# Two projections of a transformer layer by Strassen's identity, on one Trainium2 core

## The chip, the core and the metric

The kernel runs on one core of one Trainium2 chip. TensorE (PE) does the matrix products into PSUM; VectorE (DVE), ScalarE (ACT) and GpSimd (POOL) do everything elementwise; SyncE (SP) issues the weight DMAs. The metric is device microseconds of one execution of the whole layer, as a median over runs. All numbers are fp32 or fp32r.

## The reference

One layer on x of 512 rows and 1024 columns. The front part of it (three kinds of attention and gating, with their gates) is not touched by the change; what matters is the two projections behind it, each followed by a residual sum and a layer norm:

```python
merged = gates_a * (oa @ w_proj_a) + gates_b * (ob @ w_proj_b) + gates_c * (oc @ w_proj_c)
y = merged @ w_out                                   # 512x1024 @ 1024x1024
h = layer_norm(ALPHA * x + y, ln1_g, ln1_b)
a, bval = split(h @ w_ffn_up, 2)                     # 2816 columns each
a = causal_conv3(a, conv_w) + conv_b
y = (gelu(a) * bval) @ w_ffn_down                    # 512x2816 @ 2816x1024
out = layer_norm(ALPHA * h + y, ln2_g, ln2_b)
```

## The kernel before

**Splits.** Every product is computed from operands that are split into a high part (rounded, on ACT) and a low part (the rest, on DVE), and is the sum of three matmuls: high by low, low by high, high by high (`mm3_ops` L214, `mm3` L220). One step of 128 contraction rows, 128 output rows and 512 output columns is therefore three matmuls.

**The weight stream.** `emit_load` (L108) issues a DMA of 1 MB on SP into one of three raw buffers; `emit_split` (L119) makes `wh` on ACT (L133) and `wl` on DVE (L134) for units of 1024 values per partition, and `unit()` (L141) asks for them two units ahead. The left operand stands transposed in SBUF (contraction on the partitions): `m` for the output projection, split at L775 (`mTh`) and L776 (`mTl`) as each of its eight tiles is merged; for the down projection `h2`, split in `up_end` (L902) as each of its 22 tiles is made.

**Projections.** `project` (L816) holds all eight PSUM banks: 4 row blocks of 128 rows by 2 column halves. The early contraction steps run over all eight banks with one unit of weight; the last six steps (`last_rows` L798) are kept split in SBUF (`lh`, `ll`), so that the row blocks finish one after the other. Behind each block DVE adds the product to the residual (L838, `h`), takes statistics (L846, L847), POOL computes the power -0.5 (L649), and four DVE operations of 512 columns finish the norm (L851, L855). After the first projection each block of `h` is then transposed on PE (`th`, L873) and split into `hTh` and `hTl`, which the up projection multiplies (`up`, then `pa` and `pb`). After the second one each block is stored.

**Order.** The order of instructions on each engine is set ahead of time by a scheduler that works from its own times; on the chip each engine runs its list strictly in order, and waits on semaphores where an operand is not there.

Of the kernel before, what the change touches and what calls it, by code (L numbers as in the profile page):

```python
# [19 lines left out]
P = 128  # L20
# [29 lines left out]
def bucket_rows():  # L50
    """Per dilation group the bucket (one-hot, rows 0-31) and the mask (row 32) of each diagonal."""
# [18 lines left out]
def layer_kernel(  # L70
# [6 lines left out]
    big = ctx.enter_context(tc.tile_pool(name="big", bufs=17))  # L77
    wraw = ctx.enter_context(tc.tile_pool(name="wraw", bufs=3))
# [15 lines left out]
    # ---------------------------------------------------------------- weight stream  # L94
# [11 lines left out]
    raws = {}  # L106

    def emit_load():  # L108
# [4 lines left out]
        t = wraw.tile([P, 2048], F32, tag="raw", name=f"raw{n}")  # L113
# [5 lines left out]
    def emit_split():  # L119
# [4 lines left out]
        while state["load"] <= n:  # L124
            emit_load()
        src = f(raws[n])
        a = src.shape[1]
# [7 lines left out]
        prepared[u] = (h3, l3)  # L135
        state["split"] += 1
# [4 lines left out]
    def unit():  # L141
# [5 lines left out]
        while state["load"] <= min(n + 2, len(loads) - 1):  # L147
            emit_load()
        return prepared.pop(u)
# [5 lines left out]
    def kcols(w, k0, nk, c0, nc_):  # L155
        """Rows k0*128.., a [128, nk, nc_] load in units of 1024 per partition."""
# [36 lines left out]
    def krows(w, k, split):  # L193
        add_load([P, 2, 1024], w[k * P:(k + 2) * P, :].rearrange("(k p) c -> p k c", p=P),
                 [lambda r: r[:, 0:1, :], lambda r: r[:, 1:2, :]] if split else [])

    LAST = 6
    n_wout = len(loads) + (KD - LAST) // 2
    for k in range(0, KD, 2):
        krows(wo, k, k < KD - LAST)  # L200
# [9 lines left out]
    n_wdn = len(loads) + (NF - LAST) // 2  # L210
    for k in range(0, NF, 2):
        krows(wdn, k, k < NF - LAST)

    def mm3_ops(ps, w, v, first, last):  # L214
        """ps += w.T @ v for operands split into (hi, lo)."""
# [13 lines left out]
    # ---------------------------------------------------------------- x, transposed and split  # L229
# [41 lines left out]
    # ---------------------------------------------------------------- small parameters  # L271
# [62 lines left out]
    # ---------------------------------------------------------------- q, k, v  # L334
# [87 lines left out]
    # ---------------------------------------------------------------- attention pieces  # L422
# [527 lines left out]
```

## Time and profile before

| what | value |
| --- | --- |
| median of 3 runs | 822.05 us (822.04 to 822.73) |
| span of the profiled execution | 820.5 us |
| busy: PE, DVE, ACT, POOL | 807.0, 382.5, 284.4, 20.4 us |
| output projection on PE | 405.3 to 450.9 us |
| down projection on PE | 693.1 to 812.7 us |

The page gives of the profiled execution only its span; the median of the runs is 1.55 us longer, since some time lies around the span. Rows of the trace have microseconds from the start of the span. PE's busy time counts overlapped matmuls, so the distance from start to start is what a matmul costs.

### The profile page before, as it was taken

Reading aid. Unit: us, or ns where it says so; the run is one execution under the profiler, and the core shown is the slowest. Engines: PE = TensorE matmul, PEld = TensorE weight load, DVE = VectorE, ACT = ScalarE, POOL = GpSimd, SP = SyncE. Lnnn points to the kernel's source line nnn. Section 1 sums busy time; section 2 is a strip of 40 time slices with the busy share of each in tenths; the row PEclk is TensorE's granted clock in tenths of the full one; section 3 lists DMA queues with packets and bytes.
Section 4 is the critical chain, followed back from the end, with each engine's and each line's share of the span. In section 5 each row is a group of like instructions: output and inputs, shape, how many; then the busy total and the mean of one; then the engine's idle time right before and its main releaser. Section 6 shows DMA issues by size and latency. Waiting matters only on the chain.

```text
span 820.5 us, 9700 instructions
## 1 busy us (share of the span) xinstructions
PE 807.0 (98%) x4051; PEld 675.0 (82%) x4051; DVE 382.5 (47%) x591; ACT 284.4 (35%) x433; POOL 20.4 (2%) x32
## 2 busy tenths in 40 slices
PE   7999999999999999999999999999999999999996
PEld 6878997778877788888888988888888888888884
DVE  4333235836664334335856455544454445225055
ACT  4331246665365222223611243333333333224000
POOL 2001000100000000000000000000000000000000
PEclk9999999999999999999999999999999999999998
DMA  9355331122402133242840023233333324224002
GB/s 317 124 196 182 103 129 52 52 78 82 150 26 78 52 103 128 78 152 89 323 154 1 1 103 102 103 103 103 103 103 102 103 83 131 94 102 154 1 26 77
DMA packets 62411, 87.10 MB, mean 106 GB/s; under 512 B 1994, under 2 KB 50154, under 8 KB 62368
## 3 DMA queue, kind: packets, MB, share of 16 engines
q1 hardware_dynamic: 60960, 82.32, 29.5%
q0 software_dynamic: 1408, 4.17, 1.5%
q8 instruction: 32, 0.52, 0.3%
q14 instruction: 11, 0.09, 0.0%
HBM read 84.36 MB, written 4.47 MB: 108 GB/s over the span
## 4 chain that ended last, share of the span: by engine, by line
PE 98%; DMA 1%; DVE 0%; SPq 0%; issue 0%; DVEq 0%
PE y L220 20%; PE gate L220 16%; PE pa L220 13%; PE pb L220 13%; PE qk L220 7%; PE zb L220 6%; PE proj L220 5%; PE v L220 4%; PE up L220 3%; PE oT L524 1%; PE sc L524 1%; PE qc L220 1%; PE pt L493 1%; PE qk L362 1%; PE vc L220 1%; PE kc L220 1%
## 5 line engine op out<-in xcount | busy, mean ns | idle before, releaser
L134 DVE TENSOR_TENSOR wl<-raw,wh 128x1024 fp32r<-128x1024 f32 (+1 forms) x127 | 154.1, 1214 | 186.5 <-ACT wh L133 177.7
L133 ACT ACTIVATE wh<-raw 128x1024 fp32r<-128x1024 f32 (+1 forms) x127 | 133.2, 1050 | 192.9 <-PE pb L220 47.2
L220 PE MATMUL y<-wh,h 128*128 128x512 f32 x256 | 79.0, 389 | 0.0
L220 PE MATMUL gate<-xTh,wl 128*128 128x512 f32 x192 | 76.7, 400 | 0.0
L220 PE MATMUL gate<-xTh,wh 128*128 128x512 f32 x192 | 75.0, 390 | 0.0
L220 PE MATMUL gate<-xTl,wh 128*128 128x512 f32 x192 | 74.9, 390 | 0.0
L220 PE MATMUL pa<-hTh,wl 128*128 128x512 f32 x160 | 62.3, 389 | 0.0
L220 PE MATMUL pa<-hTl,wh 128*128 128x512 f32 x160 | 62.3, 389 | 0.0
L220 PE MATMUL pa<-hTh,wh 128*128 128x512 f32 x160 | 62.2, 389 | 0.0
L220 PE MATMUL pb<-hTh,wl 128*128 128x512 f32 x160 | 62.2, 389 | 0.0
L220 PE MATMUL pb<-hTl,wh 128*128 128x512 f32 x160 | 62.2, 389 | 0.0
L220 PE MATMUL pb<-hTh,wh 128*128 128x512 f32 x160 | 62.2, 389 | 0.0
L220 PEld LDWEIGHTS y<-wh,h 128*128 128x128 f32 x256 | 48.0, 188 | 10.1
L220 PE MATMUL y<-wl,h 128*128 128x512 f32 x128 | 49.8, 389 | 0.0
L898 DVE SCALAR_TENSOR_TENSOR c<-pa,par,c 128x511 f32<-128x511 f32 x20 | 15.0, 750 | 65.8 <-ACT c L897 65.8
L220 PEld LDWEIGHTS gate<-xTh,wl 128*128 128x128 f32 x192 | 36.1, 188 | 8.6 <-issue 1.2
L220 PEld LDWEIGHTS gate<-xTh,wh 128*128 128x128 f32 x192 | 36.0, 188 | 7.8
L897 ACT ACTIVATE c<-pa,par 128x512 f32<-128x512 f32 x20 | 15.6, 781 | 76.1 <-PE pa L220 76.1
L220 PEld LDWEIGHTS gate<-xTl,wh 128*128 128x128 f32 x192 | 36.1, 188 | 7.0
L220 PE MATMUL qk<-xTh,wl 128*128 128x512 f32 (+1 forms) x96 | 35.8, 374 | 0.0
L220 PE MATMUL qk<-xTh,wh 128*128 128x512 f32 (+1 forms) x96 | 35.7, 371 | 0.0
L220 PE MATMUL qk<-xTl,wh 128*128 128x512 f32 (+1 forms) x96 | 35.6, 372 | 0.0
(219 smaller groups left out, 1480.8 us busy)
## 6 DMA issues: line engine op xcount, KB each, us to landing
raw<-in_w_ffn_up SPq DMA_DIRECT2D x22, 1024.0 KB, 4.9
raw<-in_w_in SPq DMA_DIRECT2D x13, 1024.0 KB, 5.0
raw<-in_w_gate SPq DMA_DIRECT2D x12, 1024.0 KB, 5.0
raw<-in_w_ffn_down SPq DMA_DIRECT2D x11, 1024.0 KB, 4.7
raw<-in_w_out SPq DMA_DIRECT2D x4, 1024.0 KB, 4.7
shear<-vecs POOLq DMA_DIRECT2D x1, 2304.0 KB, 14.1
raw<-in_w_mem_kv SPq DMA_DIRECT2D x2, 1024.0 KB, 5.3
raw<-in_w_proj_b SPq DMA_DIRECT2D x4, 512.0 KB, 3.3
```

The costliest lines, as they stand in the source:

```text
L133: nc.scalar.activation(h3, src, AF.Copy)
L134: nc.vector.tensor_tensor(l3, src, h3.bitcast(F32), op=ALU.subtract)
L220: nc.tensor.matmul(ps, w, v, start=first, stop=last)
L362: nc.tensor.matmul(ps[:, sl], w[a][:, k, :], xs(k0 + k, sl)[c], start=k0 + i + k == 0, stop=k0 > 0 and i == 2 and k == 3)
L493: nc.tensor.transpose(pt[:, kb, u, :], self.p[:, u, kb * P:(kb + 1) * P], ident)
L524: nc.tensor.matmul(ps, w, v, start=first, stop=last)
L897: nc.scalar.activation(c, pa, AF.Identity, bias=CB(i), scale=CW(2, i))
L898: nc.vector.scalar_tensor_tensor(c[:, 1:], pa[:, :S - 1], CW(1, i), c[:, 1:], op0=ALU.mult, op1=ALU.add)
```

## The change

Both projections are computed with seven products of half-size quarters instead of eight (Winograd's form of Strassen's identity). The left operand A is cut into quarters by rows (0 to 255, 256 to 511) and by contraction (even and odd blocks of 128); the weight B by the same contraction and by columns (0 to 511, 512 to 1023). `PHASES` lists the seven products, each a left quarter or sum (S1 to S4) by a weight quarter or sum (T1 to T4); `a`, `d` and `e` are pairs of PSUM banks that sum up over phases and are added into `h` with a plus or minus sign as the phases end (`done`, L902, `add`, L900).

The weight sums are made in place on POOL (L234 to L243) in operations of 128x1024, before the split into `wh` and `wl` (L142, L143). Two of the left sums are made on POOL when the left operand is ready (`left_sums`, L824 and L825), the others are updates on DVE (L835, L838). The left operand is no longer split as it is produced: each unit in each phase splits its own left quarter into `ah` (ACT, L287) and `al` (DVE, L289 or L291), 512 values per partition. Instead of 64 steps the output projection has 56 (168 matmuls for 192), and the down projection 154 for 176 (462 for 528). The weights are loaded whole by quarters; the raw buffers come from the pool `big`, which has 20 buffers for 17, and the separate pool of three goes. Operations of 512 columns that add a bank into `h` are 14 for each projection instead of 8.

```diff
-    mTh = [T8(f"mTh{i}", F32R) for i in range(2)]
-    mTl = [T8(f"mTl{i}", F32R) for i in range(2)]
+    PHASES = (
+        ("a", "A11", "B11"), ("d", "S1", "T1"), ("a", "S2", "T2"), ("d", "S4", "B22"),
+        ("a", "S3", "T3"), ("e", "A12", "B21"), ("a", "A22", "T4"),
+    )
...
+            if q == "T1":
+                t = quarter("B11", j, n)
+                nc.gpsimd.tensor_tensor(t, t, quarter("B12", j, n), op=ALU.add)
...
+                def left_parts(u, left=left, j=j, n=n):
+                    src, scale = lefts[name](left, j, n)
+                    ah = work.tile([P, 2, 256], F32R, tag="ah", bufs=3, name=f"ah{u}")[:, :n, :]
+                    al = work.tile([P, 2, 256], F32R, tag="al", bufs=3, name=f"al{u}")[:, :n, :]
+                    split_of(ah, al, src, scale)
...
+    def left_sums(t, z, n):
+        nc.gpsimd.tensor_tensor(z, left_block(t, "A21", n), left_block(t, "A22", n), op=ALU.subtract)
+        nc.gpsimd.tensor_tensor(left_block(t, "A21", n), left_block(t, "A11", n), left_block(t, "A21", n),
+                                op=ALU.subtract)
...
+            if q == "S2":
+                nc.vector.tensor_tensor(z, z, left_block(t, "A11", n), op=ALU.subtract)
+            if q == "S4":
+                nc.vector.tensor_tensor(z, z, left_block(t, "A12", n), op=ALU.add)
...
-        for b in range(NB):
-            for hf in range(2):
-                for k in range(nk - LAST, nk):
-                    step(b, hf, k, rows[k - nk + LAST])
-                nc.vector.scalar_tensor_tensor(H(b)[:, zs], H(b)[:, zs], ALPHA, py[b][hf],
-                                               op0=ALU.mult, op1=ALU.add)
-            norm_in(b)
+        def done(ph, i):
+            a, d, e = (banks[q][i] for q in "ade")
+            if ph == 0:
+                add(i, lo, a, ALU.add, ALPHA)
+            elif ph == 1:
+                add(2 + i, hi, d, ALU.add, ALPHA)
+            elif ph == 2:
+                add(i, hi, a, ALU.subtract, ALPHA)
+            elif ph == 3:
+                add(i, hi, d, ALU.add)
+            elif ph == 4:
+                add(2 + i, hi, a, ALU.subtract)
+            elif ph == 5:
+                add(i, lo, e, ALU.add)
+                norm_in(i)
+            else:
+                add(2 + i, lo, a, ALU.add, ALPHA)
+                norm_in(2 + i)
```

**Where instructions move.** First PE, from the output projection to the up projection. Before, the transposes of one block (`th`, eight matmuls) follow each finished row block, and only those of the third block stand between the last `y` and the first `up`:

```order
L220 MATMUL y_3207<-lh,mTl_1850 128x512
L220 MATMUL y_3207<-ll,mTh_1848 128x512
L220 MATMUL y_3207<-lh,mTh_1848 128x512
L873 MATMUL th<-ident,h_3190 128x128 x8
L220 MATMUL up_3559<-hTh_3196,wl_3215 128x256
L220 MATMUL up_3559<-hTl_3198,wh_3214 128x256
```

After, behind the last matmuls into the bank `ya`, all three blocks' transposes stand ahead of `up` (`h_3175` holds blocks 0 and 1, `h_3176` blocks 2 and 3):

```order
L933 MATMUL ya_3187<-wh_3446,ah_3450 128x512
L933 MATMUL ya_3187<-wh_3446,al_3451 128x512
L933 MATMUL ya_3187<-wl_3447,ah_3450 128x512
L933 MATMUL ya_3187<-wh_3446,ah_3450 128x512
L979 MATMUL th<-ident,h_3175 128x128 x16
L979 MATMUL th<-ident,h_3176 128x128 x8
L284 MATMUL up_3616<-hTh_3182,wl_3505 128x256
L284 MATMUL up_3616<-hTl_3184,wh_3504 128x256
```

So 24 transposes stand where 8 stood, and none lies within the product.

Second DVE, at the end of the output projection. Before, one block's steps follow one another, each block behind its own two banks; this is the third block:

```order
L838 SCALAR_TENSOR_TENSOR h_3190<-h_3190,y_3204 128x512
L846 BN_STATS st<-h_3190 128x6
L838 SCALAR_TENSOR_TENSOR h_3190<-h_3190,y_3205 128x512
L846 BN_STATS st<-h_3190 128x6
L225 TENSOR_TENSOR hTl_3198<-th,hTh_3196 128x4x128
L847 BN_AGGR mv<-st 128x2
L225 TENSOR_TENSOR hTl_3199<-th,hTh_3197 128x4x128
L648 TENSOR_SCALAR mv<-mv 128x1
L851 SCALAR_TENSOR_TENSOR h_3190<-h_3190,mv,ln_3191 128x512 x2
L855 SCALAR_TENSOR_TENSOR h_3190<-h_3190,mv,ln_3191 128x512 x2
L838 SCALAR_TENSOR_TENSOR h_3190<-h_3190,y_3206 128x512
L846 BN_STATS st<-h_3190 128x6
```

After, the list from the add of the bank `ye_3190` begins with these rows; `raw_3294` and `raw_3427` are weights of the up projection:

```order
L900 SCALAR_TENSOR_TENSOR h_3175<-h_3175,ye_3190 128x512
L143 TENSOR_TENSOR wl_3505<-raw_3294,wh_3504 128x1024
L952 BN_STATS st<-h_3175 128x6 x2
L900 SCALAR_TENSOR_TENSOR h_3175<-h_3175,ye_3191 128x512
L143 TENSOR_TENSOR wl_3509<-raw_3427,wh_3508 128x1024
L953 BN_AGGR mv<-st 128x2
L952 BN_STATS st<-h_3175 128x6
L952 BN_STATS st<-h_3176 128x6
L712 TENSOR_SCALAR mv<-mv 128x1
L957 SCALAR_TENSOR_TENSOR h_3175<-h_3175,mv,ln_3177 128x512 x2
L143 TENSOR_TENSOR wl_3597<-raw_3294,wh_3596 128x1024
L900 SCALAR_TENSOR_TENSOR h_3176<-h_3176,ya_3186 128x512
```

and it goes on, ten rows later, to the split of the second block's transposed columns (`hTl`, the third and fourth of the rows with that name):

```order
L289 TENSOR_TENSOR hTl_3185<-th,hTh_3183 128x4x128
L961 SCALAR_TENSOR_TENSOR h_3175<-h_3175,mv,ln_3177 128x512 x2
L953 BN_AGGR mv<-st 128x2
L712 TENSOR_SCALAR mv<-mv 128x1
L957 SCALAR_TENSOR_TENSOR h_3176<-h_3176,mv,ln_3177 128x512 x2
L712 TENSOR_SCALAR mv<-mv 128x1
L957 SCALAR_TENSOR_TENSOR h_3176<-h_3176,mv,ln_3177 128x512 x2
L961 SCALAR_TENSOR_TENSOR h_3176<-h_3176,mv,ln_3177 128x512
L289 TENSOR_TENSOR hTl_3184<-th,hTh_3182 128x4x128
L961 SCALAR_TENSOR_TENSOR h_3176<-h_3176,mv,ln_3177 128x512
L289 TENSOR_TENSOR hTl_3185<-th,hTh_3183 128x4x128
L961 SCALAR_TENSOR_TENSOR h_3176<-h_3176,mv,ln_3177 128x512 x2
```

The adds, statistics and norms of all four blocks and four weight splits are now mixed in one stretch behind `ye_3190`.

Third POOL. Before, it has nothing to do but the powers for the norms once its first DMAs are issued:

```order
L312 DMA bias<-shear 128x4x128 x2
L396 DMA ws<-in_w_spatial 128x8x128
L649 TENSOR_TENSOR mv<-mv,mhalf 128x1 x12
L946 UNCONDITIONAL_BRANCH
```

After, this stands between the front part and the up projection (`raw` of B11 is 2998, of B12 3082, of B22 3197, of B21 3247):

```order
L713 TENSOR_TENSOR mv<-mv,mhalf 128x1 x4
L824 TENSOR_TENSOR z_out<-m_1842 128x512
L825 TENSOR_TENSOR m_1842<-m_1842 128x2x256
L234 TENSOR_TENSOR raw_2998<-raw_2998,raw_3082 128x1024 x2
L240 TENSOR_TENSOR raw_3082<-raw_3082,raw_3197 128x1024 x2
L237 TENSOR_TENSOR raw_2998<-raw_2998,raw_3197 128x1024 x2
L824 TENSOR_TENSOR z_out<-m_1843 128x512
L243 TENSOR_TENSOR raw_2998<-raw_2998,raw_3247 128x1024
L825 TENSOR_TENSOR m_1843<-m_1843 128x2x256
L243 TENSOR_TENSOR raw_2998<-raw_2998,raw_3247 128x1024
L713 TENSOR_TENSOR mv<-mv,mhalf 128x1 x4
```

Nine rows of sums are new here, and 30 more of the same kind stand in the down projection and ahead of it.

Fourth DVE at the end of the program, behind the last matmul into `ya` (5181 is row block 2, 5182 row block 3):

```order
L900 SCALAR_TENSOR_TENSOR h_3176<-h_3176,ya_5181 128x512
L900 SCALAR_TENSOR_TENSOR h_3176<-h_3176,ya_5182 128x512
L952 BN_STATS st<-h_3176 128x6 x3
L953 BN_AGGR mv<-st 128x2 x2
L712 TENSOR_SCALAR mv<-mv 128x1
L957 SCALAR_TENSOR_TENSOR h_3176<-h_3176,mv,ln_5178 128x512 x2
L712 TENSOR_SCALAR mv<-mv 128x1
L957 SCALAR_TENSOR_TENSOR h_3176<-h_3176,mv,ln_5178 128x512 x2
L961 SCALAR_TENSOR_TENSOR h_3176<-h_3176,mv,ln_5178 128x512 x4
```

Before, the steps of the last block stood there alone; now those of two blocks are interleaved.

## Rows read from the trace of the kernel before

**Rows 1.** Page, parts 1 and 4: busy time; shares of the chain.

```profile
PE 807.0 (98%) x4051; PEld 675.0 (82%) x4051; DVE 382.5 (47%) x591; ACT 284.4 (35%) x433; POOL 20.4 (2%) x32
...
PE 98%; DMA 1%; DVE 0%; SPq 0%; issue 0%; DVEq 0%
```

**Rows 2.** Chain that ended last: start us, us, engine, tile, line, count.

```profile
405.33 27.66 PE y L220 x122
...
433.86 8.19 PE y L220 x36
...
451.53 8.64 PE up L220 x72
...
693.05 119.69 PE y L220 x528
```

**Rows 3.** Timeline of PE at the boundary: start us, us, instructions.

```profile
450.49 1.03 PE L873 MATMUL th<-ident,h 128*128 128x128 f32 x8
451.28 0.36 PE L220 MATMUL up<-hTh,wl 128*128 128x256 f32 x1
```

**Rows 4.** DVE by line and form: busy us, mean ns, idle us before.

```profile
L134 DVE TENSOR_TENSOR wl<-raw,wh 128x1024 fp32r<-128x1024 f32 x125 | 152.7, 1223 | 180.0 <-ACT wh L133 171.1 <-PE tm L677 8.6
...
L851 DVE SCALAR_TENSOR_TENSOR h<-h,mv,ln 128x512 f32<-128x512 f32 x16 | 11.2, 745 | 0.0
L846 DVE BATCH_NORM_STATS2 st<-h 128x6 f32<-128x512 f32 x16 | 11.1, 694 | 0.6
...
L838 DVE SCALAR_TENSOR_TENSOR h<-h,y 128x512 f32<-128x512 f32 x16 | 11.0, 685 | 44.2 <-PE y L220 44.2
...
L776 DVE SCALAR_TENSOR_TENSOR mTl<-m,mTh 128x512 fp32r<-128x512 f32 x8 | 5.5, 689 | 3.5 <-ACT mTh L775 3.5
...
L225 DVE TENSOR_TENSOR hTl<-th,hTh 128x512 fp32r<-128x512 f32 x8 | 5.3, 668 | 5.4 <-ACT hTh L223 5.2
...
L847 DVE BATCH_NORM_AGGREGATE mv<-st 128x2 f32<-128x12 f32 x8 | 1.6, 205 | 0.2
```

**Rows 5.** Timeline of DVE, weight splits and the first norm of the output stage.

```profile
411.84 2.36 DVE L134 TENSOR_TENSOR wl<-raw,wh 128x1024 fp32r<-128x1024 f32 x2 [0.38 <-ACT wh L133]
...
424.41 0.69 DVE L838 SCALAR_TENSOR_TENSOR h<-h,y 128x512 f32<-128x512 f32 x1 [2.66 <-PE y L220]
...
426.18 1.41 DVE L851 SCALAR_TENSOR_TENSOR h<-h,mv,ln 128x512 f32<-128x512 f32 x2
427.50 1.40 DVE L855 SCALAR_TENSOR_TENSOR h<-h,mv,ln 128x512 f32<-128x512 f32 x2
```

**Rows 6.** Busy PE, PEld, DVE, ACT, POOL; granted clock; behind the last matmul.

```profile
815.00:817.00 2.00, 0.00 (x0) 0.00 (x0) 2.00 (x4) 0.00 (x0) 0.68 (x1) 0.72 0.00 0
817.00:821.00 4.00, 0.00 (x0) 0.00 (x0) 0.26 (x1) 0.00 (x0) 0.00 (x0) 0.50 0.34 131
```

**Rows 7.** Timeline of PE, the last matmul of the program.

```profile
812.34 0.39 PE L220 MATMUL y<-lh,h 128*128 128x512 f32 x1
```

**Rows 8.** Timeline of DVE behind the last matmul.

```profile
812.77 0.69 DVE L838 SCALAR_TENSOR_TENSOR h<-h,y 128x512 f32<-128x512 f32 x1 [2.33 <-PE y L220]
...
815.86 1.41 DVE L855 SCALAR_TENSOR_TENSOR h<-h,mv,ln 128x512 f32<-128x512 f32 x2
```

**Rows 9.** Page part 6, DMA issues: count, KB each, median us to landing.

```profile
raw<-in_w_ffn_down SPq DMA_DIRECT2D x11, 1024.0 KB, 4.7
```

**Rows 10.** POOL by line and form, the two tensor operations that bound a sum.

```profile
L649 POOL TENSOR_TENSOR mv<-mv,mhalf 128x1 f32<-128x1 f32 x12 | 11.2, 932 | 739.2 <-DVE mv L648 739.2
...
L248 POOL TENSOR_SCALAR_AFFINE_SELECT maskT<-maskT 128x128 f32<-128x128 f32 x1 | 0.3, 313 | 0.0
```

**Rows 11.** Timeline of POOL, two of the power operations beside busy DVE.

```profile
158.26 0.99 POOL L649 TENSOR_TENSOR mv<-mv,mhalf 128x1 f32<-128x1 f32 x1 [4.23 <-DVE mv L648]
426.40 0.92 POOL L649 TENSOR_TENSOR mv<-mv,mhalf 128x1 f32<-128x1 f32 x1 [267.15 <-DVE mv L648]
```

**Rows 12.** Timeline of DVE beside the first of these.

```profile
158.10 0.74 DVE L659 SCALAR_TENSOR_TENSOR vg<-vg,mv,sgb 128x512 f32<-128x512 f32 x1
```

More of the change, by code (lines that the diff above doesn't have):

```diff
@@ L125, in emit_split, with weight_parts @@
             emit_load()
+        if n in whole:
+            prepared[u] = f(u)
+            state["split"] += 1
+            return
         src = f(raws[n])
+        a = src.shape[1]
+        prepared[u] = weight_parts(u, src)
+        state["split"] += 1
+    def weight_parts(u, src):
         a = src.shape[1]
@@ L134, in emit_split @@
         nc.vector.tensor_tensor(l3, src, h3.bitcast(F32), op=ALU.subtract)
-        prepared[u] = (h3, l3)
-        state["split"] += 1
+        return h3, l3
     AHEAD = 2
@@ L148, in unit @@
             emit_load()
+        for v in sorted(waiting):
+            name, g, left_parts = waiting[v]
+            if g < there[name]:
+                prepared[v] += left_parts(v)
+                del waiting[v]
         return prepared.pop(u)
@@ new lines, in layer_kernel, with add_seven, quarter, weight_operand @@
+    lefts, waiting, there = {}, {}, {"out": 0, "down": 0}
+    def add_seven(name, w, nk):
+        pairs = nk // 2
+        w4 = w.rearrange("(j k p) c -> k p j c", k=2, p=P)
+        at = {}
+        for q in ("B11", "B12", "B22", "B21"):
+            r, c = int(q[1]) - 1, int(q[2]) - 1
+            for g in range(0, pairs, 4):
+                n = min(4, pairs - g)
+                at[q, g // 4] = len(loads)
+                whole.add(len(loads))
+                loads.append(([P, n, 512], w4[r][:, g:g + n, c * 512:c * 512 + 512]))
+        def quarter(q, j, n):
+            return raws[at[q, j // 4]][:, j % 4:j % 4 + n, :]
+        def weight_operand(q, j, n):
+            if q == "T1":
+                t = quarter("B11", j, n)
+                nc.gpsimd.tensor_tensor(t, t, quarter("B12", j, n), op=ALU.add)
+            elif q == "T2":
+                t = quarter("B11", j, n)
+                nc.gpsimd.tensor_tensor(t, t, quarter("B22", j, n), op=ALU.add)
+            elif q == "T3":
+                t = quarter("B12", j, n)
+                nc.gpsimd.tensor_tensor(t, t, quarter("B22", j, n), op=ALU.add)
+            elif q == "T4":
+                t = quarter("B11", j, n)
+                nc.gpsimd.tensor_tensor(t, t, quarter("B21", j, n), op=ALU.add)
+            else:
+                t = quarter(q, j, n)
+            return t
+        needs = {"B11": "B11", "T1": "B12", "T2": "B22", "B22": "B22", "T3": "B22", "B21": "B21", "T4": "B21"}
+        for bank_, left, right in PHASES:
+            for j in range(0, pairs, 2):
+                n = min(2, pairs - j)
+                def left_parts(u, left=left, j=j, n=n):
[3 more added lines that the diff above has]
+                    split_of(ah, al, src, scale)
+                    return ah, al
+                def f(u, right=right, j=j, n=n, left_parts=left_parts):
+                    waiting[u] = (name, j // 2, left_parts)
+                    return weight_parts(u, weight_operand(right, j, n))
+                units.append((at[needs[right], j // 4], f))
@@ L209, in layer_kernel @@
             units.append((n + 1, lambda r, c=c: r[:, :, c:c + 128]))
-    n_wdn = len(loads) + (NF - LAST) // 2
-    for k in range(0, NF, 2):
-        krows(wdn, k, k < NF - LAST)
+    add_seven("down", wdn, NF)
     def mm3_ops(ps, w, v, first, last):
@@ L795, in layer_kernel @@
     merge(*late)
-    def last_rows(n):
-        rows = []
-        for k2 in range(LAST // 2):
-            while state["load"] <= n + k2:
-                emit_load()
-            h = T8("lh", F32R).rearrange("p (k a) c -> p k (a c)", k=2)
-            l = T8("ll", F32R).rearrange("p (k a) c -> p k (a c)", k=2)
-            for k in range(2):
-                split_of(h[:, k, :], l[:, k, :], raws[n + k2][:, k, :])
-                rows.append((h[:, k:k + 1, :], l[:, k:k + 1, :]))
-        return rows
     hx = [T8(f"h{i}").rearrange("p (b a) c -> p b (a c)", b=2) for i in range(2)]
```

103 lines of the change are left out of this document (66 added, 37 removed).

## The prediction

> **What bounds the kernel now.** I read the page's busy times and chain shares first. PE is busy 807.0 of 820.5 us and holds 98% of the chain that ended last [rows 1]: whatever shortens PE's list shortens the run, as long as PE is fed. The chain in order of time then gives the prices: the down projection is one unbroken piece of 528 matmuls in 119.69 us, so 226.7 ns each; the output projection begins at 405.33 and `up` at 451.53 [rows 2]. The timeline of PE shows how little the norm costs at that boundary: eight transposes from 450.49, `up` from 451.28 [rows 3]. The row blocks finish some 8.2 us apart (36 matmuls in 8.19 us [rows 2]), so the norm of each runs on DVE while PE multiplies for the next. DVE as a whole is busy 47% [rows 1], which looks like room; the stages that change have to be read by themselves.
>
> **What goes.** 24 matmuls of the output projection and 66 of the down projection: 90 x 226.7 ns = 20.4 us (5.4 and 15.0), all of it on the path.
>
> **The boundary to the up projection.** In the new list of PE the transposes of three blocks stand between the last `ya` and the first `up`. They wait for three norms, and these can't begin early: the identity completes all four row blocks only in its last two phases. The output stage begins at 405.33 as before. At its start the first `al` stands behind late merges and two weight splits in DVE's list; by hand PE waits 2.0 us there. Then 168 matmuls at 226.7 ns end at 405.33 + 2.0 + 38.1 = 445.4. The bank `ye_3190` is done 30 matmuls (6.8 us) before that, at 438.6, and from its add DVE has to work through its list as far as the fourth `hTl` before `up` can run. I counted that list: 4 adds, 7 statistics, 14 norm operations and 4 splits `hTl`, all 512 wide, 4 weight splits of 1024, and 8 small ones. By themselves the 512-wide ones take 668 to 745 ns and a `wl` 1223 [rows 4], but back to back they overlap a little: from the first pair of norm operations (426.18) to the next (427.50) is 1.32 us, 0.66 each, and two `wl` take 2.36 us, 1.18 each [rows 5]. So 29 x 0.66 + 4 x 1.18 + about 1.0 for the small ones = 24.8 us, and `up` starts near 463.5 instead of 451.53: 12.0 us later, with the 5.4 us of matmuls already credited. PE stands idle for 18 us, which it never did here before.
>
> That idle has a second price. After the program's last matmul the granted clock is at 0.72 over 815 to 817 us and at 0.50 from 817 on [rows 6], the lower of its two levels, 1.2 GHz; the last matmul began at 812.34 [rows 7]. So `up` will begin at the lower level. For how long, no row shows: between nothing and the whole first piece of `up` at half speed, which is 8.64 us again [rows 2]. I take 2, nearer to nothing, as a piece of some microseconds at half speed loses about that.
>
> **Inside the down projection.** PE saves 15.0. Against it stand three waits, worked out by walking the lists of PE and DVE against each other with the durations above: 1.2 us in the third phase, where a `wl` comes late behind the updates of z; 1.7 us in the last phase, where `al` and `wl` of the last groups stand behind the statistics and norms of blocks 0 and 1 in DVE's list; and the tail. Before, the tail is one add, one statistics and four norm operations, from 812.77 to 817.27 [rows 8], 4.5 us. In the new list the adds of blocks 2 and 3 stand next to each other, the second waits for the last matmul, and behind it come three statistics and eight norm operations: 12 x 0.66 and small ones with the power between, 8.4: +3.9. So the stage gives -15.0 + 1.2 + 1.7 + 3.9 = -8.2.
>
> What costs nothing: the weight DMAs. A 1 MB load lands 4.7 us after its issue [rows 9], the 20 buffers of `big` release each load no later than before, and a stage reads its quarters over 37 us or more; if that cover went, one load would cost up to its 4.7. The removed `m` and `h2` splits (0.69 us each on DVE [rows 4]) lay beside matmuls and return nothing. ACT's splits `ah` are beside DVE's `al` and shorter than DVE's list of the same unit.
>
> Without anything else the sum is +12.0 + 2.0 - 8.2 = +5.8, made against the profiled span of 820.5; the 1.55 us between span and median stay, so 822.05 + 5.8 = 828.
>
> **The sums on GpSimd.** What T1 to T4 cost is not in the trace of before, since POOL does no wide operation there. Bounds come from the nearest rows: DVE's operation of the same shape with two inputs takes 1.22 us [rows 4], and POOL's widest, 128 columns with one input, takes 0.313 us [rows 10], eight of which are 2.5. Without an order of precedence between the two I take 2.2, nearer to POOL's own row; a left sum of 512 takes half, 1.1. The Trainium skill, page "GPSIMD Engine Reference", section "Performance versus the Vector engine", gives 4497 ns for an add of 2048 fp32 against 2293 on DVE; halved, that is an estimate of 2.25 us, and no run here shows it yet.
>
> The rows also speak of whether POOL and DVE can work at once. A power on one column takes 0.93 us [rows 10]. The one that starts at 158.26 ends at 159.25, 0.41 us after a DVE operation with two inputs in SBUF that ran from 158.10 to 158.84 [rows 11, 12]; the one that starts at 426.40 ends at 427.32, 0.40 us after the first operation of DVE's pair from 426.18, which by a mean of 0.745 [rows 4] ends at 426.92. So POOL seems to get its operands only when DVE's operation is over. DVE's own operation is not longer beside a power: the pair from 426.18 takes 1.41, the next 1.40 [rows 5]; but a power holds its operand for a moment only. I take it that a wide sum on POOL and a DVE operation with two SBUF inputs exclude each other, so that their times add. The Trainium skill, page "SBUF — State Buffer", section "Who interferes with whom", says just this: a DVE instruction with two SBUF inputs contends with a GpSimd instruction that reads SBUF, and the one that issues second waits for the whole of the first. For POOL's wait the rows above agree; for DVE's none here shows it. By that rule the sum below holds, and without it the 828.
>
> Every `wl`, `al` and update of z has two inputs in SBUF. I number the phases 0 to 6. In the output stage the second group of phase 1, the first to use a left sum of the upper half of `m`, stands behind six weight sums and three left sums on POOL, 6 x 2.2 + 3 x 1.1 = 16.5 us, and 9.9 us of two-input work on DVE; added from 399.1, when by my walk DVE begins with the stage's first weight unit, this gives 425.5, against 416 in the same walk where the two overlap: +9.5. In the first three phases of the down projection DVE has 16.5 `wl` x 1.18, 16.5 `al` x 0.66 and 5.5 updates x 0.66 = 34.0, less 1.8 done ahead: 32.2; POOL has T1, T3 and T2, 16.5 units less the two that run ahead, 14.5 x 2.2 + 1.1 = 33.0. Together 65.2 us, where PE needs the last of these splits after 41.8: +23.4. T4 beside phases 3 to 5 adds 5.5 x 2.2 = 12.1 to some 33 of DVE, 1.4 over PE's 44. Sum +34.3, on 828: **862**. With 1.22 per sum the same working gives +2.3, +8.7 and 0, so 839; with 2.5 it gives +11.8, +27.8 and +3.1, so 871.
>
> **The rivals.** One: the times don't add, since POOL reads while DVE does, or takes turns at little loss. For it speaks that DVE's pair beside a power is not longer; against it, POOL's end 0.40 us after DVE's in each case. The time is 828, from 826 with no price for the clock to 835 with all of it; lower still if the small waits inside the stages close. Two, on the other side: DVE clears the boundary fast. Place: the list from `ye_3190` to the fourth `hTl`. To break even, `up` must start by 457.7, so that list may take 19 us and not 24.8, with no contention. At the earliest, `up` starts at about 452.5, as the third block's own add, norm, transposes and split can't be shorter than 7 us behind 445.4; then the stage costs +1, the down projection -15.0 + 3.9, and the time is 812. For it speaks that statistics and small operations may overlap more; against it, that DVE's rows stand at 0.66 us in every stretch I looked at. Three: GpSimd is slower than any row bounds, or its ordered sums make DVE wait for ones it doesn't need; above 880.
>
> **How the numbers follow.** Contention 0.62, with its own range 839 to 872, at 862. No contention 0.22, at 828, of which 0.03 within 0.2%. Fast boundary 0.09. Above 880 0.07. A difference within 0.2% (1.6 us) is what a measurement of this kernel can't tell from none. Faster by more than that: the fast boundary, 0.08. Same: 0.01 of it and 0.03 of the second case, 0.04. Slower: 0.88. The range 824 to 880 leaves out the fast boundary, a little of no contention, and the worst.
>
> **What would show it.** In the profile after: 90 matmuls fewer than the 4051; an idle stretch of PE before the first `up`, 18 us without contention, ended by the transposes, with DVE busy through it; a granted clock below 1 where `up` begins; POOL's T rows with a mean near 2.2 us, longer where `wl` runs beside them; `wl` and `al` longer than 1.22 and 0.69 where POOL sums, or POOL's sums stretched by DVE; idle of PE in phases 0 to 2 of the down projection, ended by `wl`; a tail of 11 to 12 us behind the last matmul. The prediction is wrong if the matmuls of the down projection run unbroken at 226.7 ns, or if `up` starts before 457 us.

## The result, and the profile after

The changed kernel takes 872.82 us (median of 4, 871.43 to 873.48) against 822.39 for the kernel before on the same chip: 1.0611 times as long, with a 95% interval of 1.0596 to 1.0626. The forecast was 862, in a range of 824 to 880.

First the page of the profile after, busy times and chain shares. It answers to [rows 1].

```profile
PE 807.8 (93%) x3961; PEld 668.3 (77%) x3961; DVE 492.7 (57%) x671; ACT 321.7 (37%) x485; POOL 131.1 (15%) x80
...
PE 82%; DVE 14%; issue 2%; DMA 1%; ACT 1%; SPq 0%; DVEq 0%; ACTq 0%
```

PE multiplies 90 times less and is busy as long as before, since part of its matmuls ran at the lower clock (the mean granted clock of the span is 0.964 for 0.997); its share fell from 98% to 93%, and DVE holds 14% of a chain in which its share was 0%. The span is 869.7 us, 49.2 more than before. The next table splits it at five instructions of PE in the timelines: the first matmul of the output projection, its last, the first `up`, the first matmul of the down projection, its last. The last column is the run without weight sums, which is told below.

| stretch, us | before | after | after without weight sums |
| --- | --- | --- | --- |
| front part, up to the output projection | 405.17 | 408.05 | 409.33 |
| output projection | 45.48 | 51.73 | 39.96 |
| idle ahead of `up` | 0.63 | 16.84 | 17.50 |
| `up` to the end of the up projection | 241.61 | 242.89 | 242.21 |
| down projection | 119.84 | 136.82 | 104.88 |
| behind the last matmul | 7.77 | 13.37 | 12.22 |
| span | 820.5 | 869.7 | 826.1 |

**Contention.** The form groups of DVE after (line, operation, output and input, count; then busy us, mean ns of one, idle us before). They answer to [rows 4].

```profile
L143 DVE TENSOR_TENSOR wl<-raw,wh 128x1024 fp32r<-128x1024 f32 x156 | 211.9, 1361 | 132.7 <-ACT wh L142 123.8 <-PE tm L741 8.6
L289 DVE TENSOR_TENSOR al<-z_down,ah 128x512 fp32r<-128x512 f32 x15 | 21.6, 1438 | 0.9 <-ACT ah L287 0.9
...
L835 DVE TENSOR_TENSOR z_down<-z_down,h 128x512 f32<-128x512 f32 x5 | 10.9, 2179 | 0.0
L900 DVE SCALAR_TENSOR_TENSOR h<-h,ya 128x512 f32<-128x512 f32 x16 | 10.7, 678 | 1.2 <-PE ya L933 1.2
```

And POOL's weight sums, the same columns:

```profile
L237 POOL TENSOR_TENSOR raw<-raw,raw 128x1024 f32<-128x1024 f32 x7 | 20.4, 2917 | 5.3 <-DVE wl L143 5.3
...
L234 POOL TENSOR_TENSOR raw<-raw,raw 128x1024 f32<-128x1024 f32 x7 | 19.4, 2774 | 13.1 <-DVE wl L143 13.1
```

A `wl` took 1223 ns in [rows 4] and 1361 now, over all 156; an `al` on z, expected at 0.69, takes 1.44, an update of z 2.18. The add from PSUM (`L900`), which has one input in SBUF, stays at 678. How one of the long ones comes about is seen at the start of the output stage. POOL first (start us, us, instruction):

```profile
404.73 4.74 POOL L240 TENSOR_TENSOR raw<-raw,raw 128x1024 f32<-128x1024 f32 x2
410.64 2.74 POOL L237 TENSOR_TENSOR raw<-raw,raw 128x1024 f32<-128x1024 f32 x1 [1.17 <-DVE wl L143]
414.54 2.72 POOL L237 TENSOR_TENSOR raw<-raw,raw 128x1024 f32<-128x1024 f32 x1 [1.16 <-DVE wl L143]
```

and DVE at the same time:

```profile
407.50 3.07 DVE L143 TENSOR_TENSOR wl<-raw,wh 128x1024 fp32r<-128x1024 f32 x1
410.49 0.68 DVE L862 TENSOR_TENSOR m<-m,gt 128x512 f32<-128x512 f32 x1
411.09 0.68 DVE L861 SCALAR_TENSOR_TENSOR gt<-gt,proj 128x512 f32<-128x512 f32 x1
411.69 2.78 DVE L143 TENSOR_TENSOR wl<-raw,wh 128x1024 fp32r<-128x1024 f32 x1
...
414.99 2.82 DVE L291 SCALAR_TENSOR_TENSOR al<-m,ah 128x512 fp32r<-128x512 f32 x1
```

Two T3 sums that no two-input operation disturbs until 407.50 take 4.74, 2.37 each. The `wl` that starts at 407.50 ends at 410.57, 1.10 us after them: it waited, and then took its own time. The `wl` from 411.69 ends at 414.47, 1.09 after the sum that ends at 413.38, and that sum had started at 410.64. So DVE waits for POOL as POOL waited for DVE's operation in [rows 11, 12]. The two operations in between keep their 0.68 us. `L861`, from 411.09, reads one of its inputs from PSUM and runs within the sum. `L862`, from 410.49, has both inputs in SBUF, but began first: here it is the sum of 410.64 that takes 2.74 us and not 2.37. Operations with one input in PSUM go by beside sums later as well; DVE

```profile
745.98 0.68 DVE L900 SCALAR_TENSOR_TENSOR h<-h,ya 128x512 f32<-128x512 f32 x1
...
748.74 0.68 DVE L900 SCALAR_TENSOR_TENSOR h<-h,ya 128x512 f32<-128x512 f32 x1
```

beside POOL

```profile
744.94 3.33 POOL L237 TENSOR_TENSOR raw<-raw,raw 128x1024 f32<-128x1024 f32 x1
748.24 2.82 POOL L240 TENSOR_TENSOR raw<-raw,raw 128x1024 f32<-128x1024 f32 x1
```

run in 0.68 us within sums of 2.8 to 3.3. The phase of the down projection in which this does most is the second, S1 by T1. PE's matmuls that waited there:

```profile
740.04 0.79 PE L933 MATMUL yd<-wh,al 128*128 128x512 f32 x1 [2.44 <-DVE al L289]
...
748.88 0.54 PE L933 MATMUL yd<-wh,al 128*128 128x512 f32 x1 [3.35 <-DVE al L289]
...
757.72 0.80 PE L933 MATMUL yd<-wh,al 128*128 128x512 f32 x1 [4.24 <-DVE al L289]
...
767.81 0.50 PE L933 MATMUL yd<-wh,al 128*128 128x512 f32 x1 [1.98 <-DVE al L289]
```

The waits are for `al` each time, and the granted clock is low there; the window from 737 to 745 us (us, busy PE, PEld, DVE, ACT, POOL, then the clock) reads

```profile
737.00:745.00 8.00, 5.57 (x14) 3.79 (x12) 7.97 (x4) 1.58 (x2) 8.00 (x5) 0.50 0.00 0
```

at the lower level, with DVE and POOL busy throughout. By the starts of the phases (719.51, 740.04, 772.52, 789.75, 811.13) the first four last 20.5, 32.5, 17.2 and 21.4 us where 66 matmuls at 226.7 ns want 15.0. Over the first three PE is busy for 54.58 of 70.24 us, at a mean granted clock of 0.85; without the sums it needs 44.88 and waits for nothing. So of the 25.4 us lost there, 15.7 are waits and 9.7 are matmuls that took longer.

**The boundary.** PE's transposes ahead of `up`, which answer to [rows 3]:

```profile
463.53 1.97 PE L979 MATMUL th<-ident,h 128*128 128x128 f32 x8 [3.75 <-DVE h L961]
470.42 1.97 PE L979 MATMUL th<-ident,h 128*128 128x128 f32 x8 [4.92 <-DVE h L961]
474.59 2.38 PE L979 MATMUL th<-ident,h 128*128 128x128 f32 x8 [2.20 <-DVE h L961]
```

Each block's eight wait for a norm operation of DVE's list. The granted clock in that stretch, and after `up` has begun (us, busy PE, PEld, DVE, ACT, POOL, then the clock):

```profile
463.00:470.00 7.00, 1.97 (x8) 1.57 (x8) 7.00 (x13) 1.19 (x2) 0.99 (x1) 0.50 0.88 293
480.00:487.00 7.00, 7.00 (x61) 7.00 (x60) 0.00 (x0) 0.00 (x0) 0.00 (x0) 1.00 0.00 0
```

It is 0.50 in the wait, the lower level of 1.2 GHz, and at 1.00 from 480 us: the lower level costs 1.3 us in the table's fourth row, and 0.6 in the run without sums. The tail behind the last matmul, on DVE, answers to [rows 8]:

```profile
856.62 1.28 DVE L900 SCALAR_TENSOR_TENSOR h<-h,ya 128x512 f32<-128x512 f32 x2
...
862.60 2.74 DVE L961 SCALAR_TENSOR_TENSOR h<-h,mv,ln 128x512 f32<-128x512 f32 x4
```

The adds of blocks 2 and 3 come as a pair, and four norm operations stand at the end where two stood.

**The front.** One loss stands where nothing seemed to change. Page part 6 has for the front's weights

```profile
raw<-in_w_in SPq DMA_DIRECT2D x13, 1024.0 KB, 10.9
```

and of before

```profile
raw<-in_w_in SPq DMA_DIRECT2D x13, 1024.0 KB, 5.0
```

so 10.9 us from issue to landing for 5.0. The windows from 15 to 30 us of after and of before (us, busy PE, PEld, DVE, ACT, POOL, clock, DMA share, GB/s)

```profile
15.00:30.00 15.00, 12.02 (x92) 11.36 (x91) 7.96 (x10) 7.15 (x10) 0.00 (x0) 1.00 1.09 386
```

```profile
15.00:30.00 15.00, 15.00 (x107) 14.04 (x106) 8.58 (x10) 7.35 (x10) 0.00 (x0) 1.00 0.66 226
```

show PE busy 12.02 for 15.00. With twenty buffers for raw weights more loads go out at once, 386 GB/s for 226 in this window, and those that are wanted first land later; the run with a raw pool of its own, below, puts this to the test.

### The profile page after: what moved, and what is told of

Read it like the earlier page. It is cut to its first block, busy times and chain, and to the rows that moved or that the text cites. A ratio compares the mean times of both kernels' runs of the same rounds, so it can differ in the third digit from the quotient of the medians.

```text
span 869.7 us, 9778 instructions
## 1 busy us (share of the span) xinstructions
PE 807.8 (93%) x3961; PEld 668.3 (77%) x3961; DVE 492.7 (57%) x671; ACT 321.7 (37%) x485; POOL 131.1 (15%) x80
## 4 chain that ended last, share of the span: by engine, by line
PE 82%; DVE 14%; issue 2%; DMA 1%; ACT 1%; SPq 0%; DVEq 0%; ACTq 0%
PE gate L284 15%; PE pa L284 13%; PE pb L284 13%; PE qk L284 7%; PE zb L284 5%; DVE wl L143 5%; PE ya L933 5%; PE proj L284 5%; PE v L284 4%; DVE al L289 3%; PE up L284 3%; PE ye L933 2%; PE yd L933 2%; PE oT L588 1%; PE sc L588 1%
## 5 line engine op out<-in xcount | busy, mean ns | idle before, releaser
L143 DVE TENSOR_TENSOR wl<-raw,wh 128x1024 fp32r<-128x1024 f32 (+1 forms) x165 | 222.4, 1351 | 138.6 <-ACT wh L142 129.5
L142 ACT ACTIVATE wh<-raw 128x1024 fp32r<-128x1024 f32 (+1 forms) x165 | 169.2, 1029 | 154.8 <-PE pb L284 47.2
L933 PE MATMUL ya<-wh,al 128*128 128x512 f32 x120 | 47.4, 402 | 10.2 <-DVE al L291 6.9
L933 PE MATMUL ya<-wl,ah 128*128 128x512 f32 x120 | 48.0, 400 | 1.5 <-DVE wl L143 1.4
L933 PE MATMUL ya<-wh,ah 128*128 128x512 f32 x120 | 47.8, 398 | 0.0
L933 PE MATMUL yd<-wh,al 128*128 128x512 f32 x60 | 27.9, 466 | 17.6 <-DVE al L289 14.9
L824 POOL TENSOR_TENSOR z_down<-h 128x512 f32<-128x512 f32 (+1 forms) x6 | 7.2, 1198 | 218.0 <-DVE h L1010 218.0
L879 ACT ACTIVATE gt<-gate,gb 128x512 f32<-128x512 f32 x24 | 16.4, 684 | 63.6 <-PE gate L284 62.4
## 6 DMA issues: line engine op xcount, KB each, us to landing
raw<-in_w_in SPq DMA_DIRECT2D x13, 1024.0 KB, 10.9
```

What stands on the lines that cost most here:

```text
L142: nc.scalar.activation(h3, src, AF.Copy)
L143: nc.vector.tensor_tensor(l3, src, h3.bitcast(F32), op=ALU.subtract)
L824: nc.gpsimd.tensor_tensor(z, left_block(t, "A21", n), left_block(t, "A22", n), op=ALU.subtract)
L879: nc.scalar.activation(t, ps, AF.Tanh, bias=gb5[:, br * 8 + f:br * 8 + f + 1], scale=0.5)
L933: nc.tensor.matmul(ps, w, v, start=on, stop=off, skip_group_check=q in seen)
```

## The experiments

The time of before beside each of these runs was 822.1 to 822.4 us. Ratios are to it, with their 95% intervals. Theory A is that of the prediction: sums on GpSimd and two-input operations on VectorE exclude each other.

**Without the weight sums.**

```diff
             if q == "T1":
                 t = quarter("B11", j, n)
-                nc.gpsimd.tensor_tensor(t, t, quarter("B12", j, n), op=ALU.add)
```

and so for T2, T3 and T4.

> The kernel after without the weight sums: T1 to T4 are not added, the quarter that they are made in is split as it was loaded (so the two projections compute something else). Matmuls, splits, left sums, adds and lists of DVE are otherwise those of the changed kernel. Theory A (a GpSimd sum and a VectorE operation with two SBUF inputs exclude each other, so their times add): 826 to 834 us, which is my sum without contention plus what the left sums still cost, with every wl back at 1.22 us; the boundary to the up projection keeps its 12 us or more. Rival B (VectorE's own list, with al for every unit and the updates, is what starves TensorE, and the sums only lie beside it): 845 us or more.

Measured: 828.72 us, ratio 1.0078 (1.0063 to 1.0093). Its chain has the down projection as

```profile
709.16 14.96 PE ya L929 x66
...
783.96 14.29 PE ye L929 x63
```

and the phases between likewise, so 226.7 ns for each matmul, without a break. The sums cost 872.82 - 828.72 = 44.1 us, and the rest of the change 6.5; VectorE's own list is not what starves TensorE. The boundary kept its price: 17.50 us idle.

**Fills in the place of the sums.**

```diff
-                nc.gpsimd.tensor_tensor(t, t, quarter("B12", j, n), op=ALU.add)
+                for _ in range(2):
+                    nc.gpsimd.memset(t, 0.0)
```

> The kernel after with each weight sum replaced by two fills of the same tile with zero on GpSimd (so the projections compute something else): GpSimd is busy about as long, at the same place of its list, and VectorE's splits wait for it in the same way, but it reads nothing from SBUF. Theory A (it is GpSimd's reads that exclude VectorE's second input): wl and al return to 1.22 and 0.69 us beside the fills, and the time is that of the kernel without sums or up to 8 us above it, 828 to 840. Rival C (the splits are late because they wait for the result of a slow GpSimd): 860 to 873, as before, with wl short but waiting.

Measured: 828.93 us, ratio 1.0081 (1.0066 to 1.0096). DVE's `wl` and one of POOL's fills in that run:

```profile
L143 DVE TENSOR_TENSOR wl<-raw,wh 128x1024 fp32r<-128x1024 f32 x156 | 194.5, 1249 | 136.3 <-ACT wh L142 127.2 <-PE tm L745 8.6 <-DMA raw<-in_w_in 0.3
```

```profile
L247 POOL MEMSET raw<- 128x1024 f32 x14 | 13.4, 957 | 6.4 <-DVE wl L143 6.0
```

GpSimd writes to the same tiles, and VectorE's splits wait for its results, but nothing is lost: VectorE is busy for 442.3 us, as without any work there (442.6), and for 492.7 with the sums. A pair of fills takes 1.9 us, less than a sum's 2.37, so GpSimd is not busy quite as long; but the time is that without any work there, to 0.2 us, so a late result is not the cost. What is left is that a sum reads SBUF. The fills also wait for no load of the second quarter; of the sums in after, only T4's in the down projection waited for one, which the run without T4 looks at.

**The sums on VectorE.**

```diff
-                nc.gpsimd.tensor_tensor(t, t, quarter("B12", j, n), op=ALU.add)
+                nc.vector.tensor_tensor(t, t, quarter("B12", j, n), op=ALU.add)
```

> The kernel after with the 29 weight sums issued on VectorE and not on GpSimd; the left sums stay on GpSimd. Theory A: since the two exclude each other, a sum of 1.2 us on VectorE replaces 2.4 to 2.8 us of lock; by my sum +3.4 us in the output stage and +9.9 in the down projection over 828: 841, between 836 and 850. Rival D (two engines in turn are still better than one: VectorE has all the work and the sums lie on its path): 873 or more.

Measured: 845.35 us, ratio 1.0283 (1.0266 to 1.0301).

```profile
L143 DVE TENSOR_TENSOR wl<-raw,wh 128x1024 fp32r<-128x1024 f32 x156 | 194.9, 1251 | 133.7 <-ACT wh L142 124.8 <-PE tm L741 8.6
...
L237 DVE TENSOR_TENSOR raw<-raw,raw 128x1024 f32<-128x1024 f32 x7 | 8.5, 1213 | 0.0
```

A sum on VectorE takes 1.21 us and leaves `wl` at 1251 ns. (The weight sums are 32 operations and not 29: 28 of 1024 values per partition and 4 of 512.) To put the work on the engine that was already the busier of the two is worth 27 us. Done by itself, the work adds 33.0 us to VectorE's busy time (475.6 for 442.6); waiting for GpSimd to do it added 50.1.

**Blocks 0 and 1 early.**

```diff
-        ("a", "A11", "B11"), ("d", "S1", "T1"), ("a", "S2", "T2"), ("d", "S4", "B22"),
-        ("a", "S3", "T3"), ("e", "A12", "B21"), ("a", "A22", "T4"),
+        ("a", "A11", "B11"), ("e", "A12", "B21"), ("d", "S1", "T1"), ("a", "S2", "T2"),
+        ("d", "S4", "B22"), ("a", "S3", "T3"), ("a", "A22", "T4"),
...
-            if hf == 0 and i == 2:
-                turn_h(NB - 1)
+            if hf == 0 and i >= 2:
+                turn_h(i)
```

> The kernel after with the product A12 by B21 done second and not sixth, so that row blocks 0 and 1 are complete after the fifth phase and their norms lie beside two more phases; B21 is loaded a second time for T4; the transposes of blocks 2 and 3 are issued behind the first half of up. The sums stay on GpSimd. Theory A, which puts 12 us and more on the list of VectorE between the last products and up: up starts 5 to 9 us behind the last matmul of the output projection and not 25, less what later splits of up cost: 12 to 18 us saved, 854 to 861 us. Rival E (TensorE's wait there is for the last two blocks' norms, which no order of the phases takes away): no more than 5 us saved, 867 or more.

Measured: 867.26 us, ratio 1.0549 (1.0534 to 1.0565). The saving, 5.6 us, is less than half of the 12 that A expected at the least, and the number is E's (867 or more). At the place itself A holds: PE's rows there are

```profile
461.72 1.98 PE L979 MATMUL th<-ident,h 128*128 128x128 f32 x12 [0.60 <-DVE h L961]
...
467.21 0.58 PE L284 MATMUL up<-hTl,wh 128*128 128x256 f32 x1 [3.10 <-DVE hTl L289]
```

The last product ends at 460.4, and the first `up` comes 3.3 us later and not 16.8. But `up` then waits 3.1 us for the second block's split and lasts 6.0 longer in all, and the down projection lasts 141.6 us for 136.8. Of that, 2.7 us are a wait of the last product for its bank, as two products into the same bank now follow each other.

**The same without sums.** The two edits together.

> The kernel with A12 by B21 done second, as in the run with blocks early, and without the weight sums, as in the run without them (so the projections compute something else): the price of the boundary with contention out of the way. Theory A (the wait before up is VectorE's list behind the late blocks): up starts 5 to 7 us behind the last matmul of the output projection where it started 23 us behind, some of it is lost again as the second weight unit of up is split behind the norms of blocks 2 and 3; 818 to 823 us. Rival E (it is the last blocks' norms in any order): 826 or more.

Measured: 826.55 us, ratio 1.0047 (1.0031 to 1.0062), which misses A's number by 3.5 us and lies in rival E's. The trace speaks against E all the same: the gap ahead of `up` is 3.3 us for 17.5, so the list behind the late blocks was the wait. The 14.2 us that went there came back elsewhere: 3.1 at the split of block 1 and 3.2 more in `up`, 2.0 in the front, 2.4 in the output stage, and 4.7 in the down projection; the spans of the two profiles are 826.3 and 826.1. The medians are 2.2 us apart, as the profile here is of the longest of four runs and the other of the shortest. Behind the front, the two largest waits of PE in that run are

```profile
PE ya L929 <- DVE h L896: 3.5, 2, 2.8
PE up L280 <- DVE hTl L285: 3.1, 1, 3.1
```

the first of them being the add that has to empty bank `a` before the next product may go into it.

**A raw pool of its own.**

```diff
-    big = ctx.enter_context(tc.tile_pool(name="big", bufs=20))
+    big = ctx.enter_context(tc.tile_pool(name="big", bufs=17))
+    wraw = ctx.enter_context(tc.tile_pool(name="wraw", bufs=3))
...
-        t = T8(f"raw{n}").rearrange("p a b -> p (a b)")
+        if n in roomy:
+            t = T8(f"raw{n}").rearrange("p a b -> p (a b)")
+        else:
+            t = wraw.tile([P, 2048], F32, tag="raw", name=f"raw{n}")
```

(`roomy` holds the quarters other than B11.)

> The kernel after with the raw weight buffers of the front part and of B11 again in a pool of three of their own, and 17 buffers in big; only the other quarters take theirs from big. In the trace of after, the output projection begins 2.9 us later than before, since with 20 buffers the first weight loads are issued without a wait and share the DMA engines with x. Theory F (the wider pool costs these 2.9 us): the output projection begins at 405.2 again, and the time falls by about 2.7 to 3 us, to some 870. Rival: the start stays at 408 and the time at 872.8, and the loss in the front lies in something else, as the scheduler's order.

Measured: 870.32 us, ratio 1.0585 (1.0570 to 1.0599). The output projection begins at 405.06, and the window from 15 to 30 us reads

```profile
15.00:30.00 15.00, 14.98 (x105) 13.74 (x104) 8.57 (x10) 7.33 (x10) 0.00 (x0) 1.00 0.69 236
```

PE is busy 14.98 again, and the front is 3.0 us shorter; the time is 2.5 us shorter. That the two agree is in part luck: in this trace the output projection lasts 56.22 us for 51.73, with waits for `al` of 7.3 and 6.1 us where after has 6.9 and 2.7, and the down projection and the tail are 2.4 and 1.1 us shorter. The price of contention thus moves by some us when the same operations meet at other times. Nor is the front's own price one number. The seven traces with twenty buffers for all loads reach the output projection at 408.05 to 411.34 us, the four with three raw buffers at 405.06 to 405.17. In after the granted clock is 1.00 over the front; in the latest of the seven it is 0.90 from 15 to 30 us and 0.93 from 30 to 60. So the wider pool costs 2.9 to 6.2 us there, and the 2.0 us of front in the run before lie within that spread.

**Without T4 in the down projection.**

```diff
                 t = quarter("B11", j, n)
-                nc.gpsimd.tensor_tensor(t, t, quarter("B21", j, n), op=ALU.add)
+                if name == "out":
+                    nc.gpsimd.tensor_tensor(t, t, quarter("B21", j, n), op=ALU.add)
```

> The kernel after with the six sums of T4 in the down projection left out (its last product uses T2's buffer, so it computes something else), all others kept. In the trace of after these sums run as one block of 15.75 us, behind a load of B21 that comes late, and the phase beside them lasts 21.4 us for 15. Theory H (T4, which my sum put at 1.4 us because I spread it over three phases, costs its place in one phase): 5 to 7 us less, 866 to 868. If the 1.4 of my sum is right and the loss in that phase has another cause: 871 or more.

Measured: 865.33 us, ratio 1.0524 (1.0510 to 1.0539): 7.5 us less, a little beyond the 5 to 7; in the trace the down projection is 6.5 us shorter. The phase S4 by B22 lasts 15.0 us there (792.00 to 806.96) for 21.4 in after, and POOL's row in after is

```profile
793.64 15.75 POOL L243 TENSOR_TENSOR raw<-raw,raw 128x1024 f32<-128x1024 f32 x6 [23.80 <-DMA raw<-in_w_ffn_down]
```

six sums in one piece, begun when a load of B21 had landed for which POOL had waited 23.8 us.

**A version to beat both.** The output projection as before (eight products), the down projection by seven with blocks 0 and 1 early, a raw pool of three, and the weight sums made by DMAs that add into the raw buffer from HBM:

```diff
+        def plus(t, q, j, n):
+            r, c = int(q[1]) - 1, int(q[2]) - 1
+            nc.gpsimd.dma_start(t, w4[r][:, j:j + n, c * 512:c * 512 + 512], accum_op=ALU.add)
...
-    project(KD, norm1)
+    project8(KD, lambda k: (M(mTh, k), M(mTl, k)), n_wout, norm1)
```

> A version that is meant to beat both: the output projection as before (eight products), the down projection by seven with A12 by B21 second, and its weight sums made by accumulating DMAs from HBM into the raw buffers, issued on GpSimd's queue, so that no engine reads SBUF for them; raw pool of three as before. Theory A (contention is what the sums cost, VectorE's own list just keeps up): the down projection runs nearly unbroken at 226.7 ns, 15.0 us less, with a tail up to 4 us longer: 807 to 812 us. Rival B: VectorE's list with al and the updates leaves TensorE waiting, 815 or more. Rival G: the accumulating DMAs land too late for T1 or T2, which follow one another in one buffer; then TensorE waits for wl at the starts of those phases, 815 to 835.

Measured: 822.00 us (819.78 to 822.47), ratio 0.9990 (0.9981 to 0.9999). A is missed, and the time lies in the ranges of both B and G. PE waits twice in the down projection:

```profile
PE ya L979 <- DVE al L296: 3.8, 1, 3.8
PE ya L979 <- DVE h L946: 2.8, 1, 2.8
```

The first is for the split of S2 by T2: VectorE's list stood behind a `wh` on ScalarE that had itself waited 4.8 us for a DMA into the raw buffer, as the accumulates of T2 were queued behind those of T3. That is G's wait. The second is bank `a` again. The tail is 11.4 us. The next version sets the order of the accumulates and of the tail, and gives the last product banks of its own (`f`). Its edit, beside the version above:

```diff
+            after(nc.gpsimd.dma_start(t, ..., accum_op=ALU.add), "plus")
...
-        ("d", "S4", "B22"), ("a", "S3", "T3"), ("a", "A22", "T4"),
+        ("d", "S4", "B22"), ("a", "S3", "T3"), ("f", "A22", "T4"),
...
+                ins = add(2 + i, lo, f, ALU.add)
+                if i:
+                    behind(ins, lasts["norm"])
+                lasts["norm"] = norm_in(2 + i)
```

(`after` and `behind` keep the order of issue of two instructions on one engine: accumulates as written, the last product's matmuls by row block, the add of block 3 behind the norm of block 2.)

> The version with the output projection as before and the down projection by seven with accumulating DMAs, mended at the three places where its trace lost time: the accumulating DMAs of T2 are issued ahead of those of T3 (T2's landed late, TensorE waited 3.8 us); the last product has PSUM banks of its own, so it need not wait for the adds of the product before it (2.8 us); and at the end TensorE finishes row block 2 before block 3, with VectorE's norm of block 2 ahead of the add of block 3 (the tail was 4 us longer than before). Theory A: these three are worth up to 10 us, and nothing else is in the way, as the down projection without sums on GpSimd runs unbroken in 104.9 us: 810 to 815 us. Rival G (the DMA engines, saturated by the accumulates, hold up T2 or T3 whatever the order): 816 to 822.

Measured: 810.37 us (809.99 to 810.57), ratio 0.9854 (0.9837 to 0.9870), as A expected and faster than either kernel. The three changes went in together, so their shares are known from the trace alone: the down projection is 7.1 us shorter than in the version above, the tail 2.1. The down projection is

```profile
693.00 14.96 PE ya L994 x66
...
737.88 14.96 PE ya L994 x66
```

and likewise between and in the phase behind, five phases of 14.96 us without a break; the stage takes 106.6 us in all for 119.8 before. The tail on DVE

```profile
796.08 0.69 DVE L958 SCALAR_TENSOR_TENSOR h<-h,yf 128x512 f32<-128x512 f32 x1 [1.53 <-PE yf L994]
...
800.95 0.68 DVE L958 SCALAR_TENSOR_TENSOR h<-h,yf 128x512 f32<-128x512 f32 x1
...
804.03 1.41 DVE L1024 SCALAR_TENSOR_TENSOR h<-h,mv,ln 128x512 f32<-128x512 f32 x2
```

is one block's again: the span ends 9.3 us behind the last matmul, for 7.8 before.

## Why the prediction was right, and where its sizes were off

- **The matmuls that go, 15.0 us in the down projection:** exact. Without sums the stage lasts 104.88 us for 119.84.
- **The boundary, 12.0 us:** the output projection and the gap together take 68.57 us after against 46.11 before, 22.5 more. The run without sums has 57.46, so the boundary proper is +11.4, by the step as worked out: its output projection is 39.96 long, 1.9 beyond 168 matmuls, for the 2.0 of the walk, and its gap is 17.5 for 18. In after, DVE's list from the add of `ye_3190` (453.02) to the fourth `hTl` (476.39) is 23.4 us for 24.8.
- **The clock, 2.0:** 1.3, and 0.6 without sums. The granted clock fell as expected and was back at 1.00 within 4 us of the start of `up`.
- **Waits of 1.2 and 1.7 in the down projection:** wrong. Without sums there is none; the walk had DVE in the way where it was not.
- **The tail, +3.9:** 4.5 without sums, 5.6 with them.
- **Weight DMAs at nothing:** wrong, and the reason given was the wrong one to look at. Loads were released no later, but earlier, and that cost 2.9 us at the front of after, 4.2 in the run without sums.
- **Contention, +34.3:** right in kind, too small. It was 44.1. In the output stage it was 11.8 for 9.5, phases 0 to 2 of the down projection took 25.4 more than 44.9 for the 23.4, and T4 cost 6.4 to 7.5 for 1.4. Two terms were mis-sized. A sum alone takes 2.37 us where 2.2 was taken: between the prediction's own results for 2.2 and 2.5, 34.3 and 42.7, that gives an estimate of 39. And T4's sums were spread over three phases, but their operand B21 came late, so they ran as one piece beside one phase; that is most of the other 5.

So the sum's error against 872.82, 10.7 us from its unrounded 862.15, is 9.8 of contention and 0.9 of the rest. That the rest came out so near, 828.72 for 827.85, is luck: the front's loss, which the prediction put at nothing, stands against two waits that weren't there and a smaller price of the clock. The near match of contention by stage should not be pressed either, as the output projection lasted 51.73 and 56.22 us in two kernels that differ in a pool alone.

The rule of the Trainium skill, page "SBUF — State Buffer", section "Who interferes with whom", is borne out on both sides by these traces: VectorE waits for a GpSimd sum (1.22 us becomes 3.07), operations with one SBUF input go by (0.68), and fills, which read nothing, cost nothing (828.93 for 828.72). The estimate from the page "GPSIMD Engine Reference" of the Trainium skill, section "Performance versus the Vector engine", 2.25 us for a sum, is 0.12 below the trace's 2.37.

The rivals: with no contention the time would have been 828, and the kernels without sums and with fills in their place take 828.72 and 828.93; contention is the whole distance from there. The fast boundary didn't come: `up` began at 476.62, or 466.79 without sums.

What stays open is how much of the 9.7 us by which the matmuls of phases 0 to 2 took longer would come back at the higher clock, since a faster PE might only wait longer for the next `al`. Open is also what order is worth: each edit lets the scheduler set the lists anew, so differences of a few us between two of these runs may lie in that.

## What to carry to other kernels

An engine that looks idle in the shares of busy time is not free if its operations and the busy engine's exclude each other: the sums on GpSimd made VectorE 50.1 us busier, where doing them itself would have cost it 33.0. So ask of each offloaded operation how many SBUF inputs it and its neighbours have. A product with fewer matmuls that completes all its outputs in the last two of seven phases moves the work behind it out of its cover; the order of the products is part of the cost. Transfers that add as they land can take sums off both engines, if those that are wanted first are issued first. A deeper pool of buffers is not free either: here it made the first loads land later.

## What the runs showed of the hardware that was not expected

- Accumulating DMAs of 512 KB took 10.5 us from issue to landing in the last version's page (20 of them). The plain loads of 1 MB of the same weight took 9.0 us there, and those of the up projection's weight, most of which lie ahead of the accumulates, 4.9. In the version before it, the DMA engines moved some 205 GB/s from 720 to 755 us, with all of them busy. GpSimd spent 1.2 us on the issue of each.
- GpSimd and VectorE take turns in both directions, as the left sums in the up stage of after show. The sum for `z` (`L824`) from 524.71 takes 1.29 us. A `wl` from 524.96 takes 2.12 and ends 1.08 us behind it; the left sum in place (`L825`) from 526.08 takes 2.15 and ends 1.15 us behind that `wl`. With VectorE idle, the same operation in the output stage (391.34) took 1.29 us.
- In the down projection, among waits of 2 to 4 us, the granted clock read 0.50 (737 to 745 us), and a matmul behind a wait took 0.43 us from start to start for 0.227.
